# One hybrid trunk on one core: the dt weights' low and high part side by side in one product, and the decay factors of all four chunks by products of 512 columns

## The chip, the cores and the metric

The kernel is one program on one core of a Trainium2 chip. The metric is the device time of one execution in microseconds (us). The core has four engines that compute: TensorE (PE in the rows, with its weight loads shown apart as PEld), VectorE (DVE), ScalarE (ACT) and GpSimd (POOL), and SyncE (SP), which issues the transfers. Each engine works through its own list of instructions in the order in which the scheduler has put them, and waits at an instruction whose operands or whose buffer aren't ready. There are three unprofiled runs and one profiled execution.

## What is computed

The reference is a trunk of two residual layers over 1024 tokens of width 1024. Layer 0 has a state-space mixer (Mamba-2, SSD), layer 1 a causal convolution module, each is followed by a SwiGLU feed-forward part, and a last norm ends the stack. The change is in the mixer:

```python
zxbcdt = u @ w_in
z, xbc, dt = jnp.split(zxbcdt, [D_INNER, D_INNER + CONV_DIM], axis=-1)
...
dt = jax.nn.softplus(dt + dt_bias)            # 32 heads
a = -jnp.exp(a_log)
y = ssd_chunked(xs * dt[..., None], dt * a, bm, cm)
...
# in ssd_chunked, in chunks of 128 tokens
a_cs = jnp.cumsum(a, axis=-1)
lmat = jnp.exp(segsum(a))
y_diag = jnp.einsum("bgrcls,bcsgrp->bclgrp", cb[:, :, None] * lmat, x)
state_decay_out = jnp.exp(a_cs)
y_off = jnp.einsum("bclgn,bcgrpn->bclgrp", cm, states_in) * state_decay_out[..., None]
```

`dt` is one number for each head and token. `state_decay_out`, the decay factors, has to be spread over the 64 channels of a head and multiplied with what the carried state gives.

## The kernel before

All activations lie with channels on the 128 partitions and tokens along the row. The 1024 tokens are two blocks of 512 (`b` = 0, 1), and a block has four chunks of 128 (`z` = 0 to 3). A matrix product is made of rounded parts: `split` (L215) makes a high part (`hi`, by ACT) and the rest (`lo`, by DVE or POOL), and `gemm` (L237) sums `lo*hi`, `hi*lo` and `hi*hi` over slices of 128 input channels, three products of 512 columns for each slice.

The mixer runs in eight steps, one for each block and group of eight heads (`i` = 0 to 7: block `i // 4`, group `i % 4`). `ssd(i)` (L525) gives the list of a step's parts: `prep`, `A(z)` (builds the operands of chunk z and transposes its inputs, `xt`), `B(z)` (two sums of logarithms `sg` on PE, exponentials by ACT, L580, and a mask by DVE, L581, into tiles `EM`), `C(z)` (the chunk's output: state product L601, inner product L609, next state L613, then DVE steps L602 to L629), `t1` and `t2`. `weave` puts the parts of a step between the big products of the next step's input projection and the last step's output projection, so that PE has dense work between them. Out of this the framework's scheduler orders each engine's list by priority and by its own estimate of when an operand is ready.

PSUM has eight banks; in the mixer four (`mm`) hold the big products and four (`ss`) go round for everything small: `sg`, `xt`, the decay factors `eb`, `O`, `Y`, `S`. A bank that comes round again is waited for until its last reader is done.

`dt_path(b)` stands twice, for block 0 at the start and for block 1 in the fill of step 3. It loads the 1024 x 32 weights, splits them in two halves, makes 24 products of 32 output rows (8 slices x 3), multiplies by the norm's factor (block 0 alone, L400), adds the bias (L402), and turns the 32 x 512 result round by four transposes (L405), so that tokens lie on partitions; `dt_post` makes the decay exponents from it. At the start block 0's products take the inputs before the norm (`rhi_b`, `rlo_b`, made by ACT L344 and DVE L345), while the sums of squares (L254, L262) for the norm are still being made.

`decay(z)` (L584) spreads the factors of two chunks: for each of four pairs of heads one product of 256 columns whose weights are 16 rows x 128 (`self.sel`), two to a bank, and a copy by ACT of each bank into `EB` (L593). It is called twice in a step, after `B(0)` for chunks 0 and 1 and after `C(1)` for chunks 2 and 3, and both calls write the same buffer, `c_em[:, 2:4]`; `C(z)` multiplies and adds into it and reads it last at L623. The other half of `c_em` holds two of the three `EM` tiles.

## Time and profile before

| | us |
|---|---|
| three runs: median (lowest, highest) | 2513.57 (2511.85, 2514.39) |
| the profiled execution, its own time | 2513.91 |
| its span, first to last instruction | 2512.2 |
| PE busy in the span | 2488.7 (99%) |
| DVE, ACT, POOL busy | 2038.6, 1281.2, 466.0 |
| mean granted TensorE clock | 0.997 |

The mixer's eight steps take the span from about 80 to 815 us. A row of a timeline gives the start, the time of the row, engine, line, operation, the tiles written and read, rows x columns of the weights and shape, how many instructions stand merged in it, and in brackets how long the engine sat idle before it and what ended that. PE's products overlap: a row of 0.39 us may be followed by the next after 0.23 us, so the cost of a product is read from the difference of two starts. Products in plain fp32 (L601, L609, L613) have two records for each product.

### The profile page before, as it was taken

The numbers are of one execution on the slowest core, as the hardware profiler recorded it, in microseconds if no ns is written. First come the engines' busy times: TensorE is split into PE (matmuls) and PEld (weight loads), VectorE is DVE, ScalarE is ACT, GpSimd is POOL, SyncE is SP. The second block draws the span as 40 slices with busy tenths as digits, with TensorE's granted clock in tenths as the row PEclk, the third lists the DMA queues.
The fourth block names the chain that finished last, engine by engine and source line by source line (L and its number), as shares of the span: only waits on it lengthen the run. The fifth ranks groups of instructions, "written<-read, shape, count | busy, mean of one in ns | idle before, by whom it ended". The sixth has DMA issues, their size and how long they took to land.

```text
span 2512.2 us, 35442 instructions
## 1 busy us (share of the span) xinstructions
PE 2488.7 (99%) x13570; PEld 2108.8 (84%) x13570; DVE 2038.6 (81%) x2998; ACT 1281.2 (51%) x2284; POOL 466.0 (19%) x439
## 2 busy tenths in 40 slices
PE   8999999999999999999999999999999999999998
PEld 5888787887887899998888889988888899899997
DVE  7888989888889886768799578778895787986675
ACT  5665675665666554545332355452323555554443
POOL 3213312112111000000445430004444300000000
PEclk9999999999999999999999999999999999999999
DMA  4222222222223332322223242232232423332322
GB/s 141 84 72 80 76 62 76 76 80 72 76 76 100 92 107 95 109 72 93 98 94 92 95 126 99 68 101 93 98 95 89 129 91 107 130 120 81 120 80 72
DMA packets 71161, 233.50 MB, mean 93 GB/s; under 512 B 7888, under 2 KB 13264, under 8 KB 64080
## 3 DMA queue, kind: packets, MB, share of 16 engines
q1 hardware_dynamic: 70992, 231.25, 28.4%
q8 instruction: 106, 1.74, 0.3%
q14 instruction: 63, 0.52, 0.1%
HBM read 227.02 MB, written 4.19 MB: 92 GB/s over the span
## 4 chain that ended last, share of the span: by engine, by line
PE 96%; DVE 3%; ACT 1%; issue 0%; DMA 0%; POOL 0%; SPq 0%; DVEq 0%; ACTq 0%; POOLq 0%
PE p L241 68%; PE p L773 21%; PE p L609 1%; PE p L613 1%; PE p L601 1%; PE p L576 1%; PE p L564 1%; PE p L577 1%; DVE wlo L217 1%; PE p L592 0%; PE p L288 0%; PE p L544 0%; DVE h L1075 0%; DVE un_s L327 0%; DMA h<-xT 0%
## 5 line engine op out<-in xcount | busy, mean ns | idle before, releaser
L216 ACT ACTIVATE whi<-wst 128x512 fp32r<-128x512 f32 (+3 forms) x676 | 402.6, 597 | 700.4 <-PE p L241 559.5
L241 PE MATMUL p<-uhi_b,wlo 128*128 128x512 f32 x1432 | 571.6, 399 | 1.3 <-ACT uhi_b L216 1.1
L241 PE MATMUL p<-ulo_b,whi 128*128 128x512 f32 x1432 | 564.4, 394 | 1.2 <-POOL ulo_b L217 1.1
L241 PE MATMUL p<-uhi_b,whi 128*128 128x512 f32 x1432 | 562.7, 393 | 0.0
L217 POOL TENSOR_TENSOR wlo<-wst,whi 128x512 fp32r<-128x512 f32 x224 | 286.0, 1277 | 764.9 <-ACT whi L216 764.8
L241 PE MATMUL p<-hid_b,whi 128*128 128x512 f32 x1344 | 418.6, 393 | 0.0
L217 DVE TENSOR_TENSOR wlo<-wst,whi 128x512 fp32r<-128x512 f32 (+2 forms) x452 | 313.1, 695 | 109.3 <-ACT whi L216 105.7
L241 PEld LDWEIGHTS p<-uhi_b,wlo 128*128 128x128 f32 x1432 | 268.7, 188 | 67.9 <-issue 4.0
L241 PEld LDWEIGHTS p<-ulo_b,whi 128*128 128x128 f32 x1432 | 268.8, 188 | 65.4 <-POOL ulo_b L217 2.8
L773 PE MATMUL p<-uhi_b,wh_b 128*128 128x256 f32 x1728 | 323.3, 282 | 0.0
L241 PEld LDWEIGHTS p<-uhi_b,whi 128*128 128x128 f32 x1432 | 269.0, 188 | 61.9 <-issue 0.3
L241 PEld LDWEIGHTS p<-hid_b,whi 128*128 128x128 f32 x1344 | 252.5, 188 | 55.1
L773 PEld LDWEIGHTS p<-uhi_b,wh_b 128*128 128x128 f32 x1728 | 273.1, 190 | 3.2 <-ACT vw_s L800 0.8
L241 PE MATMUL p<-hid_b,wlo 128*128 128x512 f32 x672 | 264.4, 395 | 0.0
L773 PE MATMUL p<-ulo_b,wh_b 128*128 128x256 f32 x864 | 243.4, 282 | 0.0
L773 PE MATMUL p<-tu_b,wh_b 128*128 128x256 f32 x1296 | 171.6, 282 | 0.0
L773 PEld LDWEIGHTS p<-ulo_b,wh_b 128*128 128x128 f32 x864 | 163.7, 189 | 1.9
L773 PEld LDWEIGHTS p<-tu_b,wh_b 128*128 128x128 f32 x1296 | 162.7, 190 | 1.3
L987 DVE SCALAR_TENSOR_TENSOR p<-ci_b,par,p 128x499 f32<-128x499 f32 (+28 forms) x240 | 160.0, 733 | 0.9
L216 ACT ACTIVATE wh_b<-ws_b 128x1024 fp32r<-128x1024 f32 x108 | 114.3, 1060 | 88.9 <-PE p L773 38.0
L989 DVE SCALAR_TENSOR_TENSOR p<-ci_b,par,p 128x512 f32<-128x512 f32 x232 | 158.5, 749 | 0.8
L217 DVE TENSOR_TENSOR wh_b<-ws_b,wh_b 128x1024 fp32r<-128x1024 f32 x108 | 131.3, 1221 | 22.2 <-ACT wh_b L216 21.1
(238 smaller groups left out, 3936.2 us busy)
## 6 DMA issues: line engine op xcount, KB each, us to landing
wq_b<-w_gu SPq DMA_DIRECT2D x54, 1024.0 KB, 4.9
wst<-w_in SPq DMA_DIRECT2D x80, 512.0 KB, 3.5
wst<-w_gu SPq DMA_DIRECT2D x68, 512.0 KB, 3.5
wst<-w_pw SPq DMA_DIRECT2D x48, 512.0 KB, 3.5
wst<-w_dn SPq DMA_DIRECT2D x56, 384.0 KB, 3.2
wst<-w_out SPq DMA_DIRECT2D x64, 256.0 KB, 2.6
wst<-w_dn SPq DMA_DIRECT2D x32, 448.0 KB, 3.4
wst<-w_dn SPq DMA_DIRECT2D x24, 256.0 KB, 2.7
```

The source lines that it names most:

```text
L216: self.nc.scalar.activation(hi, src, AF.Copy)
L217: (eng or self.nc.vector).tensor_tensor(lo, src, hi.bitcast(F32), ALU.subtract)
L241: self.nc.tensor.matmul(acc, a, b, start=n == 0, stop=n == tot - 1)
L564: nc.tensor.transpose(xt[:, zs(j)], self.XS[i][:, j, zs(z)], self.ident)
L576: nc.tensor.matmul(sg, self.gtr, aml, start=True, stop=False)
L577: nc.tensor.matmul(sg, self.gtr, amh, start=False, stop=True)
L601: nc.tensor.matmul(O[:, zs(j)], H[:, zs(j)], CT[:, zs(z)], start=True, stop=True)
L609: nc.tensor.matmul(Y[po:po + 64, zs(hh // 2)], self.XDT[z % 2][:, hh * 64:(hh + 1) * 64], E[:, zs(r)], start=True, stop=True)
L613: nc.tensor.matmul(S, self.BTOK[:, zs(z)], self.XDD[z % 2], start=True, stop=True)
L773: nc.tensor.matmul(to, x, y, start=n == 0 and not more, stop=n == 11, skip_group_check=True)
L987: nc.vector.scalar_tensor_tensor(acc[:, s:], x[:, HALO:TW - s], w(s), acc[:, s:], op0=ALU.mult, op1=ALU.add)
L989: nc.vector.scalar_tensor_tensor(acc if s < 30 else c, x[:, HALO - s:TW - s], w(s), acc, op0=ALU.mult, op1=ALU.add)
```

## The change

For dt, the split weights lie side by side in one tile, 32 columns of low part and 32 of high part, from one ACT and one DVE instruction instead of two and two. Two products for each slice (inputs' low and high part) instead of three give 64 output rows: the upper 32 with the low weights, the lower 32 with the high weights. The factor and the bias are applied to all 64 rows (half the bias to each), and the four transposes become four products with a 64 x 32 matrix of two identities (`id2`), which add both halves. Two DVE instructions at the start make `id2` and the halved bias `hb`.

For the decay factors, `B(0)` is followed by all four pairs: four products of 512 columns, each with a bank and a copy of its own, into the whole of `c_em`. The call after `C(1)` is gone. Two of the `EM` tiles move to a tile of another pool (`em2`), given back after the mixer.

```diff
+        self.hb, self.id2 = ff[:, 1978:1979], ff[:, 1980:2012]
...
+        nc.vector.tensor_tensor(self.id2, self.ident[:, :32], self.ident[:, 32:64], ALU.add)
+        nc.vector.tensor_scalar(self.hb, self.pcol("dt_bias", 0), 0.5, None, op0=ALU.mult)
...
-        self.EM = [self.c_em[:, 0], self.c_em[:, 1], self.c_ms[:, 3]]
-        self.EB = self.c_em[:, 2:4].rearrange("p a (j z l) -> p (a j) z l", z=2, l=P)
+        self.c_e2 = self.half.new("em2")
+        e2 = self.c_e2.rearrange("p (m n) c -> p m (n c)", n=2)
+        self.EM = [e2[:, 0], e2[:, 1], self.c_ms[:, 3]]
+        self.EB = self.c_em.rearrange("p j (z l) -> p j z l", l=P)
...
         def load():
-            st["w"] = self.weight(self.io["w_dt"], 8, 32)
+            w = self.wp.tile([P, 8, P], F32, tag="wst", bufs=2, name=self.nm("wst"))
+            w = w.rearrange("p k c -> p (k c)")[:, :256].rearrange("p (k c) -> p k c", c=32)
+            nc.sync.dma_start(w, self.io["w_dt"])
+            st["w"] = self.wp.tile([P, 4, P], F32R, tag="whi", bufs=4, name=self.nm("whi"))
+            st["w"] = st["w"].rearrange("p k c -> p (k c)").rearrange("p (k c) -> p k c", c=64)
+            self.split(st["w"][:, :, 32:], st["w"][:, :, :32], w)

         def gemm():
             st["acc"] = self.bank("mm")
-            self.gemm(st["acc"][:32], st["w"], self.U[b] if u is None else u)
+            x = [y for hl in (self.U[b] if u is None else u) for y in hl[::-1]]
+            for n, y in enumerate(x):
+                nc.tensor.matmul(st["acc"][:64], st["w"][:, n // 2], y, start=n == 0, stop=n == 15)
...
-            nc.vector.tensor_tensor(raw[:32], acc[:32], fac[:32], ALU.mult)
+            nc.vector.tensor_tensor(raw[:64], acc[:64], fac[:64], ALU.mult)
...
-        nc.vector.tensor_scalar(raw[:32], acc[:32], self.par[:32, o:o + 1], None, op0=ALU.add)
+        nc.vector.tensor_scalar(raw[:64], acc[:64], self.hb[:64], None, op0=ALU.add)
...
-            nc.tensor.transpose(tp[:, z * 32:(z + 1) * 32], raw[:32, z * P:(z + 1) * P], self.ident[:32, :32])
+            nc.tensor.matmul(tp[:, z * 32:(z + 1) * 32], raw[:64, z * P:(z + 1) * P], self.id2[:64],
+                             start=True, stop=True)
...
-        def decay(z):
-
-            w = slice(z * P, (z + 2) * P)
-            for a in range(2):
+        def decay(a):
+
+            gp = slice(32 * g, 32 * g + 16)
+            for j in (2 * a, 2 * a + 1):
                 eb = self.bank("ss")
-                for j in range(2):
-                    gp = slice(32 * g, 32 * g + 16)
-                    lt = self.sel.rearrange("p q c -> p (q c)")[gp, zs(2 * a + j)]
-                    nc.tensor.matmul(eb[:, 2 * P * j:2 * P * (j + 1)], lt, self.er[gp, w], start=True, stop=True)
-                nc.scalar.activation(self.c_em[:, 2 + a], eb, AF.Copy)
+                nc.tensor.matmul(eb, self.sel.rearrange("p q c -> p (q c)")[gp, zs(j)], self.er[gp], start=True, stop=True)
+                nc.scalar.activation(self.c_em[:, j], eb, AF.Copy)
...
-            EB = self.EB[:, :, z % 2]
+            EB = self.EB[:, :, z]
...
-        steps = [prep, lambda: A(0), lambda: (B(0), decay(0)), lambda: A(1)]
+        steps = [prep, lambda: A(0), lambda: (B(0), decay(0), decay(1)), lambda: A(1)]
         for z in range(NZ):
-            steps.append(lambda z=z: (C(z), decay(2)) if z == 1 else C(z))
+            steps.append(lambda z=z: C(z))
```

On PE, at `B(0)` of step 0, the list of before has the two `sg` sums (`am_b,sr_b`), the four decay products of chunks 0 and 1 (`sr_b` alone) and then the big products of the next projection (`uhi_b`, `ulo_b`):

```order
L577 MATMUL p_92_837<-am_b_91,sr_b_65 128x512
L592 MATMUL p_93_842<-sr_b_65 128x256 x2
L592 MATMUL p_94_846<-sr_b_65 128x256 x2
L241 MATMUL p_95_850<-uhi_b_245,wlo_737 128x512
L241 MATMUL p_95_850<-ulo_b_246,whi_736 128x512
```

The list of the changed kernel at the same place, where L592 and L593 are now the sums, L605 the decay products and L244 the big products:

```order
L593 MATMUL p_89_827<-am_b_91,sr_b_65 128x512
L605 MATMUL p_90_832<-sr_b_65 128x512
L605 MATMUL p_91_835<-sr_b_65 128x512
L244 MATMUL p_94_844<-uhi_b_235,wlo_727 128x512
L244 MATMUL p_94_844<-ulo_b_236,whi_726 128x512
L605 MATMUL p_92_838<-sr_b_65 128x512
L244 MATMUL p_94_844<-uhi_b_235,whi_726 128x512
L244 MATMUL p_94_844<-uhi_b_235,wlo_727 128x512
L244 MATMUL p_94_844<-ulo_b_236,whi_726 128x512
L244 MATMUL p_94_844<-uhi_b_235,whi_726 128x512
L605 MATMUL p_93_841<-sr_b_65 128x512
L244 MATMUL p_94_844<-uhi_b_235,wlo_727 128x512
```

The four products now stand in three places between dense products: two together, one, one. So it is in six of the eight steps; in steps 3 and 7 three stand together and one apart. In the whole program the decay products stand in 22 places, in the list of before in 19.

On ACT, at the same place of step 0, before has the two exponentials (L580) with a convolution step (L483) between them, the two copies of decay factors (L593), and operands of `A(1)` and weights (`whi`) after them:

```order
L580 ACTIVATE em_b_92<-p_91_832 128x512
L483 ACTIVATE v_s_815<-sf_b_64 128x512
L580 ACTIVATE em_b_92<-p_92_837 128x512
L593 ACTIVATE em_b_92<-p_93_842 128x512
L593 ACTIVATE em_b_92<-p_94_846 128x512
L560 ACTIVATE am_b_91<-sf_b_64,sr_b_65 128x128 x2
L216 ACTIVATE whi_887<-wst_885 128x512
```

In the changed kernel the exponentials are L596 and the copies L606:

```order
L596 ACTIVATE em_x_97<-p_88_822 128x512
L499 ACTIVATE v_s_805<-sf_b_64 128x512
L596 ACTIVATE em_x_97<-p_89_827 128x512
L606 ACTIVATE em_b_92<-p_90_832 128x512
L606 ACTIVATE em_b_92<-p_91_835 128x512
L606 ACTIVATE em_b_92<-p_92_838 128x512
L606 ACTIVATE em_b_92<-p_93_841 128x512
L219 ACTIVATE whi_881<-wst_879 128x512
```

Two copies more stand ahead of the weights; the two that stood behind `C(1)` are gone.

On PE, in step 3, where block 1's dt product is, the list of before has products of 32 output rows, a pair of decay products among them, and the inner products of `C(1)` (L609):

```order
L577 MATMUL p_439_3375<-am_b_91,sr_b_65 128x512
L241 MATMUL p_469_3556<-ulo_b_3278,whi_3514 32x512
L592 MATMUL p_454_3494<-sr_b_65 128x256 x2
L241 MATMUL p_469_3556<-uhi_b_3277,whi_3514 32x512
L241 MATMUL p_469_3556<-uhi_b_3277,wlo_3515 32x512
L241 MATMUL p_469_3556<-ulo_b_3278,whi_3514 32x512
L241 MATMUL p_469_3556<-uhi_b_3277,whi_3514 32x512
L241 MATMUL p_469_3556<-uhi_b_3277,wlo_3515 32x512
L241 MATMUL p_469_3556<-ulo_b_3278,whi_3514 32x512
L241 MATMUL p_469_3556<-uhi_b_3277,whi_3514 32x512
L609 MATMUL p_451_3470<-ms_b_96,xd_b_93 64x128 x4
L609 MATMUL p_451_3470<-em_b_92,xd_b_93 64x128 x4
```

In the changed kernel (L406 the dt products, L622 the inner products) they are of 64 rows, with no decay product among them:

```order
L593 MATMUL p_438_3357<-am_b_91,sr_b_65 128x512
L406 MATMUL p_463_3525<-uhi_b_3259,whi_3488 64x512
L406 MATMUL p_463_3525<-ulo_b_3260,whi_3488 64x512
L406 MATMUL p_463_3525<-uhi_b_3259,whi_3488 64x512
L406 MATMUL p_463_3525<-ulo_b_3368,whi_3488 64x512
L406 MATMUL p_463_3525<-uhi_b_3367,whi_3488 64x512
L406 MATMUL p_463_3525<-ulo_b_3368,whi_3488 64x512
L406 MATMUL p_463_3525<-uhi_b_3367,whi_3488 64x512
L406 MATMUL p_463_3525<-ulo_b_3368,whi_3488 64x512
L592 MATMUL p_455_3491<-am_b_91,sr_b_65 128x512
L622 MATMUL p_450_3452<-ms_b_96,xd_b_93 64x128 x4
L622 MATMUL p_450_3452<-em_x_97,xd_b_93 64x128 x4
```

The inner products stand behind 13 of the 16 dt products and three of the sums, before behind 12 of the 24, two sums and a pair of decay products.

## Rows read from the trace of the kernel before

**Rows 1.** The page: busy time, share of the span and instructions of each engine; and the chain of work that ended last, its shares by engine.
```profile
PE 2488.7 (99%) x13570; PEld 2108.8 (84%) x13570; DVE 2038.6 (81%) x2998; ACT 1281.2 (51%) x2284; POOL 466.0 (19%) x439
...
PE 96%; DVE 3%; ACT 1%; issue 0%; DMA 0%; POOL 0%; SPq 0%; DVEq 0%; ACTq 0%; POOLq 0%
```

**Rows 2.** Waits of PE over the whole span: the instruction that waited, what it waited for, us in total, times, longest.
```profile
PE p L241 <- DVE rlo_b L345: 3.0, 5, 1.0
...
PE p L241 <- ACT uhi_b L216: 1.1, 1, 1.1
...
PE p L564 <- ACT em_b L593: 1.0, 1, 1.0
PE p L576 <- DVE ms_b L545: 0.9, 1, 0.9
...
PE p L592 <- DVE xd_b L570: 0.3, 1, 0.3
PE p L609 <- DVE ms_b L581: 0.3, 1, 0.3
```

**Rows 3.** Busy time by stretch of the span, all engines: the stretch and its length, PE, PEld, DVE, ACT and POOL busy (instructions), PE's granted clock (1.00 is 2.4 GHz, 0.50 is 1.2 GHz), DMA share, GB/s.
```profile
9.70:13.00 3.30, 2.84 (x6) 0.71 (x6) 3.30 (x8) 2.78 (x6) 1.54 (x1) 0.50 1.04 416
...
40.40:43.70 3.30, 3.30 (x11) 2.27 (x10) 3.08 (x6) 0.00 (x0) 2.15 (x2) 0.50 0.12 50
...
82.00:820.00 738.00, 734.91 (x3720) 587.27 (x3719) 643.16 (x958) 467.77 (x978) 154.19 (x162) 1.00 0.24 77
```

**Rows 4.** Timeline at the start: PE at three of its waits (block 0's dt product twice, the first normalized inputs once), and DVE at one step of the sum of squares.
```profile
15.59 0.42 PE L241 MATMUL p<-rlo_b,whi 128*32 128x512 f32 x1 [0.96 <-DVE rlo_b L345]
...
20.68 0.43 PE L241 MATMUL p<-rlo_b,whi 128*32 128x512 f32 x1 [0.92 <-DVE rlo_b L345]
...
39.41 0.49 PE L241 MATMUL p<-uhi_b,wlo 128*128 128x512 f32 x1 [1.14 <-ACT uhi_b L216]
...
19.27 0.69 DVE L262 TENSOR_TENSOR ssum_s<-ssum_s,sq_s 128x512 f32<-128x512 f32 x1 [1.19 <-POOL ssum_s L262]
```

**Rows 5.** Timeline of step 3: PE in block 1's dt product and at the inner products behind it, and DVE at what these waited for.
```profile
388.82 0.39 PE L241 MATMUL p<-uhi_b,wlo 128*32 128x512 f32 x1
389.05 0.40 PE L241 MATMUL p<-ulo_b,whi 128*32 128x512 f32 x1
389.28 0.39 PE L241 MATMUL p<-uhi_b,whi 128*32 128x512 f32 x1
...
390.69 0.66 PE L609 MATMUL p<-ms_b,xd_b 128*64 128x128 f32 x8 [0.32 <-DVE ms_b L581]
...
389.96 0.68 DVE L581 TENSOR_TENSOR ms_b<-ms_b 128x512 f32<-128x512 f32 x1
```

**Rows 6.** Timeline of step 3 a little later: PE at the transposes of `A(3)`, ACT at the square that stands ahead of the decay copies and at these copies, DVE at two steps of `C(1)` (L620 reads `Y`, L623 reads `EB` last).
```profile
398.20 0.66 PE L564 MATMUL p<-ident,xs_b 128*128 128x128 f32 x4 [0.97 <-ACT em_b L593]
...
397.04 0.63 ACT L627 ACTIVATE gsq_s<-sz_b 128x512 f32<-128x512 f32 x1 [1.12 <-DVE sz_b L623]
397.57 1.06 ACT L593 ACTIVATE em_b<-p 128x512 f32<-128x512 f32 x2
...
392.36 0.67 DVE L620 TENSOR_TENSOR em_b<-em_b,p 128x512 f32<-128x512 f32 x1
...
396.08 0.93 DVE L623 TENSOR_TENSOR sz_b<-sz_b,em_b 128x512 f32<-128x512 f32 x1
```

**Rows 7.** Timeline of PE around decay products: four of them in step 0, and two of them in step 7.
```profile
91.48 0.40 PE L577 MATMUL p<-am_b,sr_b 128*128 128x512 f32 x1
91.80 0.73 PE L592 MATMUL p<-sr_b 16*128 16x256 f32 x4
92.47 0.50 PE L241 MATMUL p<-uhi_b,wlo 128*128 128x512 f32 x1
92.80 0.39 PE L241 MATMUL p<-ulo_b,whi 128*128 128x512 f32 x1
93.03 0.40 PE L241 MATMUL p<-uhi_b,whi 128*128 128x512 f32 x1
...
786.01 0.40 PE L241 MATMUL p<-yl_b,whi 128*128 128x512 f32 x1
786.33 0.50 PE L592 MATMUL p<-sr_b 16*128 16x256 f32 x2
786.76 0.51 PE L241 MATMUL p<-yh_b,whi 128*128 128x512 f32 x1
787.10 0.39 PE L241 MATMUL p<-yh_b,wlo 128*128 128x512 f32 x1
```

**Rows 8.** Timeline of PE: the four transposes of dt in block 1, and the four fp32 state products of a chunk (two records each, 128 columns).
```profile
402.69 0.44 PE L405 MATMUL p<-ident,dtraw_s 32*128 32x32 f32 x4
...
112.92 1.06 PE L601 MATMUL p<-bct_b,H_b 128*128 128x128 f32 x8
```

**Rows 9.** Timeline of ACT behind the two sums of step 0: exponentials, a convolution step, copies of decay factors.
```profile
91.99 0.59 ACT L580 ACTIVATE em_b<-p 128x512 f32<-128x512 f32 x1
92.47 0.81 ACT L483 ACTIVATE v_s<-sf_b 128x512 f32<-128x512 f32 x1
93.17 0.60 ACT L580 ACTIVATE em_b<-p 128x512 f32<-128x512 f32 x1
93.65 1.09 ACT L593 ACTIVATE em_b<-p 128x512 f32<-128x512 f32 x2
```

More of the change, by code (lines that the diff above doesn't have):

```diff
@@ L384, in dt_path @@
     def dt_path(self, b, u=None, fac=None):
+        nc = self.nc
         st = {}
         def load():
-            st["w"] = self.weight(self.io["w_dt"], 8, 32)
+            w = self.wp.tile([P, 8, P], F32, tag="wst", bufs=2, name=self.nm("wst"))
[4 more added lines that the diff above has]
+            self.split(st["w"][:, :, 32:], st["w"][:, :, :32], w)
         def gemm():
             st["acc"] = self.bank("mm")
-            self.gemm(st["acc"][:32], st["w"], self.U[b] if u is None else u)
+            x = [y for hl in (self.U[b] if u is None else u) for y in hl[::-1]]
+            for n, y in enumerate(x):
+                nc.tensor.matmul(st["acc"][:64], st["w"][:, n // 2], y, start=n == 0, stop=n == 15)
         return [Unit(gemm, load), Unit(lambda: self.dt_pre(b, st["acc"], fac)), Unit(lambda: self.dt_post(b))]
@@ L1121, in run @@
             q += weave(self.ssd(i), fill) + post
-        q += [Unit(lambda: self.big.drop(*self.mix_bigs)), call(self.phase, 8)]
+        q += [Unit(lambda: (self.big.drop(*self.mix_bigs), self.half.drop(self.c_e2))), call(self.phase, 8)]
         fast = lambda *a, **k: self.ffn(*a, fast=True, **k)
```

## The prediction

> **What bounds the kernel now.** I read the page's busy times and chain first, then PE's waits, then the stretches, then the timeline at each place that the diff touches. PE is busy for 99% of the span and carries 96% of the chain that ended last [rows 1]. Between 82 and 820 us, which holds the mixer, it is busy 734.91 of 738.00 us, while DVE has 643 and ACT 468 [rows 3]. So in the mixer a product that goes away is time gained, and a change on DVE or ACT counts only where PE comes to wait for it. The list of PE's waits is short: about 3 us for `rlo_b` and 1.1 us for `uhi_b`, both at the start, and in the mixer single waits of 0.3 to 1.0 us [rows 2]. Two of these, at L564 and L592, are at the change. The exception is the start: there PE stands at 15.59 and 20.68 for DVE's `rlo_b`, and at 39.41 for ACT's `uhi_b` [rows 4].
>
> **Part 1, block 1's dt product (step 3).** Sixteen products take the place of 24. One costs 0.23 us, the difference of the starts 388.82, 389.05 and 389.28 [rows 5] with 32 columns of weights, and 0.23 with 128 (92.80 to 93.03 [rows 7]), so I take 0.23 for 64 too. Eight fewer: -1.84 us, on a path where PE has no cover to lose.
>
> **Part 2, block 0's dt product (start).** Eight fewer there as well, but PE is waiting between them: each pair of products needs one `rlo_b` from DVE, and at 15.59 and 20.68 it sat idle 0.96 and 0.92 us for it [rows 4]. DVE itself waits in the sum of squares (1.19 us at 19.27, for POOL), and that chain, not PE, leads to the norm and to the `uhi_b` for which PE waits 1.14 us at 39.41. The dropped products only lengthen idle time: 0. The two added DVE instructions (two small tiles) end before that 1.19 us of DVE idle time, which covers them; uncovered they would cost a few tenths. Bounds for the part: -1.84 (all gained) and +1.7 (the clock, rival C).
>
> **Part 3, four transposes become four fp32 products of 64 rows, twice.** The four transposes take 0.44 us as a row [rows 8]. No row has an fp32 product of 32 columns. From below: no more than now, 0. From above: as long as the four fp32 products of 128 columns, 1.06 us, so +0.62 each time. Those have two records for each product where a transpose has one. I take two passes of what is one now, about 0.06 us more for each of four, +0.25 us; twice, +0.5 us. Both stand where PE is dense afterwards.
>
> **Part 4, the decay products on PE.** A place with four products of 256 columns takes PE from 91.48 to 92.80, that is 1.32 us, of which two ordinary products are 0.46: 0.86 us. A place with two takes from 786.01 to 787.10, 1.09 less 0.46: 0.63 us [rows 7]. So two products cost 0.23 us, 0.115 each, and going into the 16-row shape and out again costs 0.40 us a place, however many stand in it (the product before is followed after 0.32 to 0.33 instead of 0.23, the first dense one after 0.34). A product of 512 columns in this shape isn't in the trace; at the least it is what dense ones take, 0.23, at the most two of 256, 0.23 also, so there is little to choose. Before: 64 x 0.115 + 19 x 0.40 = 14.96 us. After, with the 22 places that the order has: 32 x 0.23 + 22 x 0.40 = 16.16 us. That is +1.2 us. Against it goes the wait at L592 for `xd_b`, 0.35 us at most by [rows 2], which I tie to the call after `C(1)` in step 7 (its bank came round late): -0.3. Sum +0.9 us. So joining two products into one gains nothing, and scattering them loses.
>
> A rule of the Trainium skill would say otherwise of the joining: TensorEngine Tiling (Array Packing), in Performance Considerations, gives each product an overhead of some 60 cycles. As an estimate from that page, at 2.4 GHz, 32 fewer products would save 0.8 us more, and the time forecast below would be 2511.8. The rows speak against it here: two of 256 cost no more than one of 512.
>
> **Part 5, the call after `C(1)` disappears.** Its copies wrote a buffer which DVE was still reading. In step 3 they stood on ACT behind a square that waited 1.12 us for L623 (396.08 to 397.0), ran at 397.57, and PE stood at the transposes of `A(3)` 0.97 us for the bank that they emptied [rows 6]. In the new order of banks these transposes take the bank of `Y`, free after L620 at 393.0. The wait goes: -0.97 us; a further wait in its place would be for L620, and by 393.0 that is early enough. The other 0.9 us wait, at L576 for L545, is ahead of the change and stays.
>
> **Part 6, a wait that grows.** In step 3 the inner products waited 0.32 us for L581, which DVE began at 389.96, held by other work [rows 5]. With 13 instead of 12 dt products, one sum more and two pairs of decay products fewer ahead of them, PE is there some 0.8 us earlier. If L581 comes no earlier, all of that is waited: +0.8; if ACT's new order brings it forward by as much, 0. I take the middle, +0.4 us.
>
> **Part 7, ACT.** As many copies as before, but all four behind the exponentials. Two new copies of about 0.5 us (two took 1.09) stand ahead of the next weights' split, 1.1 us later at worst. The weights have two sets of buffers, and in the whole list from which [rows 2] are taken PE never waits for `whi` or `wlo`, so nothing. The third decay product needs the bank of the first sum, empty when its exponential ends at 92.58; the fourth that of the second, 93.77 [rows 9]. By the order the third comes at about 93.1 and the fourth at about 94.55, so each has 0.5 to 0.8 us to spare. Cost 0; what it takes without that cover is rival B.
>
> **Sum.** -1.84 + 0 + 0.5 + 0.9 - 0.97 + 0.4 = -1.0 us. Against the profiled execution's own 2513.91 that is 2512.9; it lies 0.34 above the median of the runs, so against 2513.57 I forecast 2512.6, 0.04% less. In step 7's end the scheduler has also cut some small groups apart and put others together; with the sizes above that is 0.8 us either way, and I leave it in the range.
>
> **Rivals.**
>
> A, the first product counts as well. For it: it is eight products, and the low clock from 40.40 to 43.70 [rows 3] comes after a stretch of waits that an earlier PE could shorten. Against: the waits there are for DVE, ACT and POOL [rows 4]. It would give -1.84 more, and half of 3.3 us, 1.65, if that low stretch goes: 2509.1, and 2508.2 with parts 3 and 6 at their lower ends. Chance 0.13.
>
> B, slower: the four banks. All four are taken by two sums and two decay products when the third and fourth come, and PE's list can't pass them; everything dense behind waits for ACT. It decides from the point where an exponential ends more than 0.5 to 0.8 us later than in [rows 9], in all steps. To end 0.2% above before it must cost 6 us, 0.75 us a step; the time would be 2519. Against it: ACT is half idle, and steps 3 and 7 have no convolution step between the exponentials. Chance 0.06.
>
> C, the clock at the start. From 9.70 to 13.00 it was granted at 0.50, with PE busy 2.84 of 3.30 us on six products before it rose [rows 3]; after the change two thirds of these remain in the same time. If it then stays at 1.2 GHz for another such stretch, 1.65 us of PE's pace are lost, of which the idle 0.96 and 0.92 us [rows 4] cover most; uncovered it is 2514.2. Chance of the uncovered price 0.13. The Trainium skill's TensorE: Matmul & The Clock Gate, Part 1, says that the low clock is the default and that activity releases it; by that rule the rise would come later after this change, and the trace agrees so far as its rise follows a busy stretch.
>
> D, the gain of step 3 doesn't last. DVE and ACT set the pace there: part 6 costs its 0.8 and another wait takes the place of part 5's 0.97: 2512.6 + 0.4 + 0.97 = 2514.0. Chance 0.15.
>
> **How the numbers follow.** My forecast has 0.53. A run of this kernel can be told from no change beyond about 0.2%, 5 us: faster is under 2508.5, slower over 2518.6. The forecast, C and D lie within. Of A, whose two times lie on both sides of the border, I count 0.08 as faster and 0.05 as within. Faster 0.12, within 0.2% 0.80, slower 0.08; 0.04 of the first and 0.02 of the last are for what I haven't thought of. The range goes down to 2508.5 (A without the lower ends) and up to 2515.5 (D with step 7's 0.8 and part 3's upper end), which leaves out some 2 in 10.
>
> **What would show it.** The dt products' rows: 16 at 0.23 us in step 3. Decay products: 32 of 512 columns with 22 places at 0.4 us over the dense pace; a place with one product at 0.63 us proves part 4, at 0.25 refutes it. L564's wait for L593 gone; L609's wait for L581 in step 3 at 0.3 to 1.1 us. At the start PE still idle at `rlo_b` and at `uhi_b` near 39.4. A wait of the decay products for the exponentials, step after step, would prove B and the forecast wrong; a granted clock of 0.50 after 13.1 us would prove C.

## The result: 0.22% slower, and runs that scatter

The changed kernel takes 2517.55 us in the median of 22 runs, the kernel before 2512.9 in 22, that is 4.65 us less. One run of the changed kernel, at 13854.28 us, is a slow one and stands outside the ratio and all that follows. The ratio of the means is 1.0022, interval 1.0016 to 1.0028. The forecast was 2512.6 with a range up to 2515.5, so the time lies outside. The runs of before lie between 2511.39 and 2514.39; those of the changed kernel begin at 2513.32 and reach 2524.7. Its nine runs above 2519 us have mean granted clocks of 0.992 to 0.994, the twelve others 0.995 to 0.998. The profiled execution took 2515.16 us, span 2513.3; it is one of the shorter ones.

The page after: busy times, and the chain by engine. PE's share of the chain falls from 96% to 94% and DVE's rises from 3% to 4% [rows 1].

```profile
PE 2490.1 (99%) x13530; PEld 2106.9 (84%) x13530; DVE 2038.8 (81%) x2998; ACT 1282.0 (51%) x2282; POOL 465.8 (19%) x439
...
PE 94%; DVE 4%; ACT 1%; issue 0%; POOL 0%; DMA 0%; SPq 0%; DVEq 0%; ACTq 0%; POOLq 0%
```

Waits of PE in the mixer after (us in total, times, longest). The waits at the transposes for the decay copies and at the decay products for `xd_b` [rows 2] are gone; 1.2 us at the next-state product (L626, which was L613 in before) and 0.6 us in step 7 have come.

```profile
PE p L626 <- DVE xd_b L586: 1.2, 1, 1.2
PE p L592 <- DVE ms_b L561: 0.9, 1, 0.9
PE p L592 <- ACT uhi_b L219: 0.6, 1, 0.6
PE p L622 <- DVE em_x L597: 0.4, 1, 0.4
```

Stretches after, columns as in [rows 3]. The clock column is what matters: in the mixer, where the trace of before has no stretch below 1.00, there is now one at 0.50, that is at 1.2 GHz. The row of the whole mixer doesn't show it: a mean over 738 us, it reads 1.00 as it did in before.

```profile
8.40:18.60 10.20, 7.94 (x17) 3.86 (x18) 9.03 (x22) 8.71 (x16) 4.40 (x2) 0.50 0.82 298
40.40:43.70 3.30, 3.30 (x19) 2.69 (x18) 3.30 (x6) 0.63 (x1) 1.77 (x4) 1.00 0.00 0
82.00:820.00 738.00, 734.47 (x3671) 582.72 (x3670) 640.78 (x953) 467.71 (x976) 152.52 (x162) 1.00 0.24 76
400.90:404.30 3.40, 2.20 (x12) 1.38 (x12) 2.42 (x5) 0.00 (x0) 0.00 (x0) 1.00 0.46 153
404.30:407.70 3.40, 3.40 (x9) 2.63 (x10) 3.28 (x8) 0.83 (x2) 0.19 (x1) 0.50 0.00 1
407.80:411.20 3.40, 3.40 (x17) 2.78 (x16) 1.95 (x3) 0.63 (x1) 0.00 (x0) 1.00 0.00 0
```

PE's timeline in step 3 around it: the second half of the inner products, one dense product, the wait, the fp32 next-state product, the turn of dt (L420), and then dense products that follow one another after 0.43 us instead of 0.23. In before, the turn of dt and this step's wait, which was then at the transposes, lay 4.5 us apart with dense products between them [rows 6, 8].

```profile
399.92 0.61 PE L622 MATMUL p<-ms_b,xd_b 128*64 128x128 f32 x8
400.46 0.49 PE L244 MATMUL p<-uhi_b,wlo 128*128 128x512 f32 x1
402.15 1.10 PE L626 MATMUL p<-xd_b,ms_b 128*128 128x512 f32 x2 [1.20 <-DVE xd_b L586]
403.18 1.08 PE L420 MATMUL p<-sf_b,dtraw_s 64*128 64x32 f32 x8
404.18 0.70 PE L244 MATMUL p<-ulo_b,whi 128*128 128x512 f32 x1
404.68 0.63 PE L244 MATMUL p<-uhi_b,whi 128*128 128x512 f32 x1
405.11 0.63 PE L244 MATMUL p<-uhi_b,wlo 128*128 128x512 f32 x1
```

The timeline of PE at the parts that were priced: two dt products of step 3, 0.23 us apart; and a decay product by itself in step 0 (compare [rows 5, 7]). From 90.92 to 92.01 are 1.09 us, less two ordinary products (0.46) 0.63 for this place.

```profile
386.12 0.39 PE L406 MATMUL p<-ulo_b,whi 128*64 128x512 f32 x1
386.35 0.40 PE L406 MATMUL p<-uhi_b,whi 128*64 128x512 f32 x1
...
90.92 0.40 PE L244 MATMUL p<-ulo_b,whi 128*128 128x512 f32 x1
91.25 0.50 PE L605 MATMUL p<-sr_b 16*128 16x512 f32 x1
91.67 0.50 PE L244 MATMUL p<-uhi_b,whi 128*128 128x512 f32 x1
92.01 0.40 PE L244 MATMUL p<-uhi_b,wlo 128*128 128x512 f32 x1
```

To see where time comes and goes I take the starts of the same dense product of projections and feed-forward in two traces (both have 12216) and subtract that of before. Numbers are us; a column is the product that starts at that time in before.

| kernel | 82 | 200 | 296 | 383 | 480 | 830 | 2499 |
|---|---|---|---|---|---|---|---|
| after | -1.87 | -1.32 | -0.91 | +0.28 | +0.74 | +0.92 | +0.93 |
| after_again | -1.37 | -0.81 | -0.25 | +0.99 | +3.14 | +3.36 | +3.47 |
| dt_both | -1.38 | -1.38 | -1.25 | -1.21 | -2.58 | -2.31 | -2.29 |
| decay_only | -1.11 | -0.58 | -0.01 | +1.20 | +0.93 | +1.14 | +1.22 |
| after_fill | -1.49 | -0.90 | +2.64 | +3.88 | +2.86 | +3.05 | +3.09 |
| plug23 | -2.55 | -1.99 | +1.69 | +2.92 | +2.48 | +2.70 | +2.75 |
| before_long | -2.25 | -2.19 | +2.09 | +2.13 | +2.15 | +2.14 | +2.28 |
| full_before | +1.09 | +0.26 | -0.24 | -0.69 | -0.61 | -3.00 | -2.60 |
| full_after | +2.76 | +3.85 | +3.38 | +3.94 | +1.80 | -0.70 | -0.60 |

Behind 830 us no row changes by more than 0.4. The columns 200 and 296 stand beside decay products that the lists place differently, so there a difference can shift by about 1.2 us from one product to the next. In after the start gains 1.9, then each stretch loses. The gain at the start is an execution's, not the change's: before_long, whose start is that of before, gains 2.25 there (by [rows 3] the low stretch at 40 us alone, missing in both, is worth up to 1.65).

### The profile page after: what moved, and what is told of

Same layout as the page of the kernel before. It is cut to its first block, busy times and chain, and to the rows that moved or that the text cites. A ratio compares the mean times of both kernels' runs of the same rounds, so it can differ in the third digit from the quotient of the medians.

```text
span 2513.3 us, 35345 instructions
## 1 busy us (share of the span) xinstructions
PE 2490.1 (99%) x13530; PEld 2106.9 (84%) x13530; DVE 2038.8 (81%) x2998; ACT 1282.0 (51%) x2282; POOL 465.8 (19%) x439
## 4 chain that ended last, share of the span: by engine, by line
PE 94%; DVE 4%; ACT 1%; issue 0%; POOL 0%; DMA 0%; SPq 0%; DVEq 0%; ACTq 0%; POOLq 0%
PE p L244 66%; PE p L786 21%; PE p L622 1%; PE p L626 1%; PE p L614 1%; DVE wlo L220 1%; PE p L592 0%; PE p L605 0%; PE p L593 0%; PE p L580 0%; PE p L291 0%; DVE v_s L501 0%; DVE un_s L330 0%; PE p L560 0%; DVE h L1088 0%
## 5 line engine op out<-in xcount | busy, mean ns | idle before, releaser
L219 ACT ACTIVATE whi<-wst 128x512 fp32r<-128x512 f32 (+2 forms) x674 | 402.4, 598 | 703.1 <-PE p L244 555.1
L244 PE MATMUL p<-uhi_b,wlo 128*128 128x512 f32 x1424 | 569.3, 400 | 1.6 <-ACT uhi_b L219 1.5
L244 PE MATMUL p<-ulo_b,whi 128*128 128x512 f32 x1424 | 561.7, 395 | 1.2 <-POOL ulo_b L220 1.1
L244 PE MATMUL p<-uhi_b,whi 128*128 128x512 f32 x1424 | 559.8, 393 | 0.0
L244 PE MATMUL p<-hid_b,whi 128*128 128x512 f32 x1344 | 418.7, 393 | 0.0
L220 DVE TENSOR_TENSOR wlo<-wst,whi 128x512 fp32r<-128x512 f32 (+1 forms) x448 | 315.6, 706 | 108.8 <-ACT whi L219 105.4
L244 PEld LDWEIGHTS p<-uhi_b,wlo 128*128 128x128 f32 x1424 | 268.1, 188 | 69.7 <-issue 7.6
L244 PEld LDWEIGHTS p<-ulo_b,whi 128*128 128x128 f32 x1424 | 267.9, 188 | 64.8 <-issue 3.3
L244 PEld LDWEIGHTS p<-uhi_b,whi 128*128 128x128 f32 x1424 | 268.0, 188 | 62.0 <-issue 1.6
L244 PEld LDWEIGHTS p<-hid_b,whi 128*128 128x128 f32 x1344 | 252.4, 188 | 55.2
L244 PE MATMUL p<-hid_b,wlo 128*128 128x512 f32 x672 | 264.4, 395 | 0.0
```

What stands on the lines that cost most here:

```text
L219: self.nc.scalar.activation(hi, src, AF.Copy)
L220: (eng or self.nc.vector).tensor_tensor(lo, src, hi.bitcast(F32), ALU.subtract)
L244: self.nc.tensor.matmul(acc, a, b, start=n == 0, stop=n == tot - 1)
```

## The experiments

"Before" is always the median of the runs of before that stood beside a kernel on its chip. The 95% interval of a ratio reaches some 0.09% to either side, 2.2 us, so a difference below that is not clear of none.

**The two parts alone, and the two dt products alone.** Edits: the lines of the change for dt without those for the decay factors (dt_both), the other way round (decay_only), and dt_both for one block:

```diff
-            w = self.wp.tile([P, 8, P], F32, tag="wst", bufs=2, name=self.nm("wst"))
+            if b != 0:    # dt_first; dt_second has 1
+                st["w"] = self.weight(self.io["w_dt"], 8, 32)
+                return
```

> The kernel before with the dt products of both blocks changed and the decay products as they were. The changed kernel's runs go from 2513.3 to 2524.7 us where those of before go from 2511.4 to 2514.4, and long runs show a lower mean granted clock. Theory S (stretches of low clock that come in some runs only, caused by the first dt product at the start) and theory U (the same, caused by the second dt product and the fp32 turn in step 3): median 2515 to 2518, runs spread over 6 us or more. Theory E (the decay products, scattered over more places, cause them): 2511.5 to 2513, spread 3 us, since eight products fewer in step 3 save 1.84 and two turns by fp32 products cost 1.3.

> The kernel before with the decay products changed and the dt products as they were. Theory E: median 2515 to 2519, runs spread over 6 us or more, mean clock down to 0.993 in the long ones. Theories S and U: 2513 to 2515 (scattering the products costs 1 to 2 us on PE), spread 3 us like before.

> The kernel before with block 0's dt product alone changed, at the start. Theory S: median 2515 to 2517, spread 6 us or more, low clock after 13 us or after 43 us in the profile. Theories U and E: 2512 to 2514, spread 3 us.

> The kernel before with block 1's dt product alone changed, in step 3. Theory U: median 2514 to 2517, spread 6 us or more, low clock between 390 and 420 us in the profile, as in the changed kernel's profile at 404.31 to 407.72. Theories S and E: 2511 to 2513 (sixteen products instead of 24 save 1.84, the fp32 turn costs 0.64), spread 3 us.

Measured, before 2513.39: dt_both 2511.99 (-1.40), decay_only 2515.39 (+2.00), dt_first 2514.12 (+0.73), dt_second 2512.32 (-1.07). No profile of the four has a low clock between 45 and 2500 us. The parts add up to +0.6, near the changed kernel's shortest runs (+0.4), and 4 us short of its median. Three of eleven runs of dt_first (2517.4 to 2517.7) and one of dt_both (2516.35) stand 2.9 and 2.2 us above the next one; the longest of decay_only (2517.6) is 2.2 above its median, as the longest run of before there is above its own. So no theory of the three has it alone: neither part has the changed kernel's scatter of 11 us, the two together have it. The same holds for the 1.2 us wait at the next-state product of step 3: it is in the profile of neither dt_both nor decay_only.

**The same kernel again; more work at the start; the turn by transposes.** after_again has no edit. after_fill:

```diff
             for n, y in enumerate(x):
+                if b == 0 and n % 2 == 0:
+                    nc.tensor.matmul(d[:64], st["w"][:, n // 2], x[n + 1], start=True, stop=True)
                 nc.tensor.matmul(st["acc"][:64], st["w"][:, n // 2], y, start=n == 0, stop=n == 15)
```

after_turn:

```diff
-            nc.tensor.matmul(tp[:, z * 32:(z + 1) * 32], raw[:64, z * P:(z + 1) * P], self.id2[:64],
-                             start=True, stop=True)
+            nc.tensor.transpose(tp[:, z * 64:(z + 1) * 64], raw[:64, z * P:(z + 1) * P], self.ident[:64, :64])
...
-        nc.vector.tensor_copy(v, tp[:, :128])
+        nc.vector.tensor_copy(v3, t4[:, :, 0])
+        nc.vector.tensor_tensor(v3, v3, t4[:, :, 1], ALU.add)
```

> The changed kernel once more, beside the others on one chip. If its scatter belongs to the kernel: median 2516 to 2519, highest above 2520, mean clock in the long runs 0.992 to 0.994. If it belonged to the executions of that other time: median 2513 to 2515 (the two parts alone sum to +0.6 us over before), highest under 2518.

> The changed kernel with eight products put back into block 0's dt product, whose result nobody reads (high weights by high inputs, into a bank of its own, ahead of each pair), so that PE is as busy at the start as before. Theory S (PE too idle at the start, low clock lasting longer there in some runs): median 2513 to 2515, spread 3 to 4 us, mean clock not under 0.996. Theory U (low clock from the fp32 turn and the wait in step 3): as the changed kernel, 2516 to 2519 with runs above 2520.

> The changed kernel with the two turns of dt by transposes of 64 rows (tokens by 64 columns) and DVE adding the halves, in place of fp32 products. By the measured 1.00 us for four fp32 products against 0.36 for four transposes it saves 1.0 to 1.3 us at the medians. Theory U: the low clock at 404 goes and the scatter with it, median 2512 to 2514. Theory S: scatter as in the changed kernel, median 2515 to 2517.

Measured, before 2513.15: 2517.20 (2515.0 to 2523.2), 2517.16 (2516.6 to 2524.1, in seven runs) and 2517.92 (2514.0 to 2520.6). The scatter belongs to the kernel. Theory S falls: with as much work at the start as before it stays. Theory U falls in its first form: without the fp32 turn it stays. The turn itself is shorter, 0.39 us from 406.93 to 407.32 against 1.00, yet the median isn't. What the three profiles give is the place: after_again has its low clock from 404.6 to 411.4, as after in step 3; the other two have it from 266.3 and 267.0 on, in step 2, for 6.8 us. The table shows the price: after_fill loses 3.5 us between 200 and 296 where after loses 0.4. Two executions of one kernel show it too: between 383 and 480, where after_again is at 1.2 GHz for 6.8 us and after for 3.4, the one loses 2.15 us and the other 0.46. The row of after_again:

```profile
404.60:411.40 6.80, 6.80 (x19) 5.47 (x19) 3.58 (x9) 1.46 (x3) 0.19 (x1) 0.50 0.06 25
```

**Filling PE's waits.** plug3 puts three dense products ahead of the waiting next-state product of step 3; plug23 also makes the first sum of `B(0)` in step 2 three times over, where PE waits 1.0 us.

```diff
                 S = self.bank("ss")
+                if i == 3 and z == 2:
+                    for _ in range(3):
+                        nc.tensor.matmul(S, self.gtr, self.U[1][0][0], start=True, stop=True)
...
-                nc.tensor.matmul(sg, self.gtr, aml, start=True, stop=False)
-                nc.tensor.matmul(sg, self.gtr, amh, start=False, stop=True)
+                for _ in range(1 + 2 * (i == 2 and z == 0 and q == 0)):
+                    nc.tensor.matmul(sg, self.gtr, aml, start=True, stop=False)
+                    nc.tensor.matmul(sg, self.gtr, amh, start=False, stop=True)
```

> The changed kernel with three dense products of 512 columns put ahead of the state product of C(2) in step 3, where PE waits 1.2 us for DVE; they write its bank, which the state product then overwrites. Theory M (a low clock follows where a PE wait stands among decay, fp32 and transposing products with hardly a dense one between; in step 3 at 400 to 404, in step 2 at 263 to 267; each takes 1.7 or 3.4 us, in runs of its own): no low clock at 404 to 412, median 2514.5 to 2516, some runs still above 2517 for step 2. Rival N (the low clock is not tied to these places): as the changed kernel, 2517 and scatter to 2523.

> The same, and the first sum of B(0) in step 2 made three times over (four more dense products where PE waits 1.0 us for DVE). Theory M: no low clock between 45 and 2500 us, median 2513 to 2515, highest under 2517. Rival N: 2517 and scatter.

Measured, before 2512.88: plug3 2518.25 (2514.5 to 2522.3), plug23 2516.23 (2513.8 to 2517.8). The first filling missed its aim: the timeline of plug3 shows that the added products themselves wait for the bank, whose last reader is DVE's L586, so the idle time stands where it stood. And yet this profile has no low clock there; it has it in step 2.

```profile
406.44 0.93 PE L628 MATMUL p<-uhi_b,sr_b 128*128 128x512 f32 x3 [1.22 <-DVE xd_b L586]
407.21 1.02 PE L629 MATMUL p<-xd_b,ms_b 128*128 128x512 f32 x2
...
267.00:273.80 6.80, 6.80 (x15) 4.36 (x15) 3.99 (x7) 1.63 (x4) 0.26 (x2) 0.50 0.14 41
404.00:411.00 7.00, 5.78 (x38) 4.10 (x35) 6.59 (x13) 1.49 (x3) 0.19 (x1) 1.00 0.23 75
```

The second filling worked, and refuted theory M. In plug23 PE has no wait in step 2 (stretches, then its timeline), and yet the clock falls, behind the decay products of 16 rows. Its scatter is half of plug3's, so the wait may still have a share.

```profile
262.90:266.30 3.40, 3.13 (x9) 1.32 (x9) 3.40 (x6) 3.07 (x6) 2.19 (x3) 1.00 0.17 60
266.40:273.10 6.70, 6.70 (x15) 4.97 (x16) 4.43 (x7) 3.83 (x11) 0.10 (x1) 0.50 0.15 39
```

```profile
263.11 0.50 PE L593 MATMUL p<-am_b,sr_b 128*128 128x512 f32 x1
263.45 0.39 PE L594 MATMUL p<-am_b,sr_b 128*128 128x512 f32 x1
263.77 1.09 PE L606 MATMUL p<-sr_b 16*128 16x512 f32 x2
264.79 0.50 PE L244 MATMUL p<-uhi_b,wlo 128*128 128x512 f32 x1
265.13 0.39 PE L244 MATMUL p<-ulo_b,whi 128*128 128x512 f32 x1
265.46 0.49 PE L606 MATMUL p<-sr_b 16*128 16x512 f32 x1
265.88 0.49 PE L244 MATMUL p<-uhi_b,whi 128*128 128x512 f32 x1
266.30 0.78 PE L606 MATMUL p<-sr_b 16*128 16x512 f32 x1
...
267.61 0.63 PE L244 MATMUL p<-ulo_b,whi 128*128 128x512 f32 x1
```

**More 16-row products in before.** In the kernel before, the four decay products of step 2's first call are made four times each.

```diff
+                    for _ in range(4 if i == 2 and z == 0 else 1):
                         nc.tensor.matmul(eb[:, 2 * P * j:2 * P * (j + 1)], lt, self.er[gp, w], start=True, stop=True)
```

> The kernel before with the four decay products of chunks 0 and 1 in step 2, behind the 0.93 us wait, made four times over each (12 more products of 256 columns and 16 rows, 1.4 us at 0.115). Theory M with 16-row products counting little for the clock: low clock behind 266 us in most runs, median 2516 to 2518, spread 4 us or more. Rival N, or 16-row products counting like dense ones: 2514 to 2515, spread 3 us.

Measured: 2514.74 (+1.86; 2512.9 to 2516.9). The median lies where rival N had it (2514 to 2515): the twelve added products alone are worth 1.4 us at 0.115, so the low clock can't have cost the median run much. The profile is of one of the two longest runs (2516.20 us). It has the low clock, in a place where no profile with before's decay products had it, and the table shows its 4.3 us between 200 and 296. It begins while the sixteen products run, which take 3.04 us, 0.19 each:

```profile
263.27 3.11 PE L593 MATMUL p<-sr_b 16*128 16x256 f32 x16
266.31 0.80 PE L241 MATMUL p<-uhi_b,wlo 128*128 128x512 f32 x1
...
260.80:264.10 3.30, 2.23 (x13) 1.39 (x12) 3.30 (x6) 2.80 (x5) 1.72 (x2) 1.00 0.28 79
264.20:270.90 6.70, 6.70 (x22) 5.51 (x21) 5.38 (x8) 3.29 (x8) 0.96 (x3) 0.50 0.12 42
```

**All four decay products in one place.** after_ahead puts them ahead of the sums; ahead_apart does so in all steps but step 2, with both fillings, the turn by transposes, and block 1's turn two projections later.

```diff
-        steps = [prep, lambda: A(0), lambda: (B(0), decay(0), decay(1)), lambda: A(1)]
+        steps = [prep, lambda: A(0), lambda: (decay(0), decay(1), B(0)), lambda: A(1)]
...
-dtp[:1] + ip[:1] + dtp[1:2] + ip[1:]
+dtp[:1] + ip[:3] + dtp[1:2] + ip[3:]
```

> The changed kernel with the four decay products ahead of the two sums of B(0) instead of behind them, so that all four of a step stand in one place: 8 places with 4 products of 512 columns instead of 22. By part 4's price (0.40 us a place, 0.23 a product) their cost falls from 17.0 to 8 x 1.32 = 10.6 us: 6.4 us less than the changed kernel on the same chip, 2509 to 2512 with its scatter. Rival: the four copies by ACT keep the banks that the sums need next, PE waits up to 0.8 us in each step, and all of it is given back: 2515 to 2518.

> The changed kernel with the decay products ahead of the sums in all steps but step 2 (10 places instead of 22), the turn by transposes, the turn of block 1 two projections later, away from C(2), and both fillings of plug23. Theory M and part 4's price: 5.8 us less for the places, 0.6 to 1.3 for the turn, no low clock in the mixer: 2506.5 to 2509, highest under 2512, so under the kernel before by 0.2% or more. Rival N: 2509 to 2513 with scatter. Against it: waits that the new places bring, as the 1.1 and 0.6 us in step 2 of the run with all steps ahead.

Measured: after_ahead 2512.99 (-0.16), that is 4.2 less than after_again beside it; ahead_apart 2511.25 (-1.63). Part 4's price holds: a place of four takes from 90.04 to 91.81, 1.77, less 0.46: 1.31 us, and 0.40 + 4 x 0.23 is 1.32. Of the 6.4 us two thirds arrive; in its profile some go into new waits, 1.3 us at L291 ahead of step 1 (0.3 in after) and 0.6 more in step 2. ahead_apart misses theory M's 2506.5 to 2509 and lies where rival N had it, and both kernels' profiles still have the low clock in step 2 (from 267.4 and 268.4).

```profile
90.04 0.39 PE L244 MATMUL p<-uhi_b,whi 128*128 128x512 f32 x1
90.36 1.19 PE L605 MATMUL p<-sr_b 16*128 16x512 f32 x4
91.48 0.50 PE L244 MATMUL p<-uhi_b,wlo 128*128 128x512 f32 x1
91.81 0.40 PE L244 MATMUL p<-ulo_b,whi 128*128 128x512 f32 x1
```

**128 rows instead of 16.** The decay products take all rows; a POOL instruction in each step sets the selection of the other groups to zero. PE's order is the same, instruction by instruction.

```diff
+            nc.gpsimd.tensor_tensor(self.selm, self.sel.rearrange("p q c -> p (q c)").bitcast(F32),
+                                    self.mask[:, g:g + 1].to_broadcast([P, 512]), ALU.mult)
...
-                nc.tensor.matmul(eb, self.sel.rearrange("p q c -> p (q c)")[gp, zs(j)], self.er[gp], start=True, stop=True)
+                nc.tensor.matmul(eb, self.selm[:, zs(j)], self.er, start=True, stop=True)
```

> The changed kernel with all decay products on 128 rows instead of 16: their weights are the same selection with zeros in the rows of the other groups (made by one POOL instruction in each step's first part), the moving operand is the whole tile. PE's order and columns are the same. Theory R (16 rows, not idle time alone, bring the low clock, and the 0.40 us of a place come from going into the 16-row shape and out): the places fall from 17.0 to 32 x 0.23 = 7.4 us, no low clock at 263 to 273, at most the one at 404 is left; median 2504 to 2507 against 2517. Theory M (the idle time alone brings the low clock, and a change of operands alone costs the 0.40): 2516 to 2518 with scatter.

> The kernel before with the decay products on 128 rows, PE's order the same. Theory R: 15.9 us for the places fall to 64 x 0.115 = 7.4, median 2504 to 2506. Theory M: 2512 to 2514.

> full_after with the turns by transposes and block 1's turn two projections later, away from C(2). Theory R and the low clock in step 3 from the gathering of fp32 products, turn and wait: 2502 to 2505, spread 4 us or less, no low clock between 45 and 2500 us. Theory M: 2513 to 2516.

> The kernel before with the dt products changed (as in dt_both, 2511.99) and the decay products on 128 rows, 256 columns, in the two calls of before. Theory R: 8.5 us less than dt_both, 2502 to 2505. Theory M: 2511 to 2513.

Measured, before 2512.73: full_after 2513.42 (+0.69, where the changed kernel has +4.0 to +4.7), full_before 2510.07 (-2.66), full_apart 2510.74 (-1.99), full_dt 2508.39 (-4.34). In the rows theory R holds: most of the places' price is gone, and the clock stays up in step 2. In the times it doesn't: all four lie below theory M's ranges, but 3.4 to 6.4 us above those of theory R. Timeline of full_after in step 2: the 1.00 us wait is still there, with all four decay products behind it, and the clock stays at 1.00; a single place in step 0 takes from 95.16 to 95.96, 0.80, less 0.46: 0.34 with a product that is itself 0.23.

```profile
268.91 0.50 PE L603 MATMUL p<-am_b,sr_b 128*128 128x512 f32 x1 [1.00 <-DVE ms_b L572]
...
269.49 0.39 PE L616 MATMUL p<-sr_b 128*128 128x512 f32 x1
270.20 0.47 PE L616 MATMUL p<-sr_b 128*128 128x512 f32 x1 [0.32 <-DVE xd_b L597]
...
95.16 0.40 PE L253 MATMUL p<-ulo_b,whi 128*128 128x512 f32 x1
95.39 0.49 PE L616 MATMUL p<-sr_b 128*128 128x512 f32 x1
95.73 0.39 PE L253 MATMUL p<-uhi_b,whi 128*128 128x512 f32 x1
95.96 0.40 PE L253 MATMUL p<-uhi_b,wlo 128*128 128x512 f32 x1
...
266.40:273.10 6.70, 5.38 (x23) 3.80 (x22) 6.70 (x11) 4.92 (x9) 3.17 (x4) 1.00 0.17 46
```

The median single place is 0.26 against 0.63 in after. In neither of the two profiles with 128 rows and the changed order (full_after, full_apart) does the clock fall in step 2; with 512-column products of 16 rows it fell there in six of nine. The other profiles with 128 rows (full_before, full_dt and two below) have the order of before, in which it stayed up with 16 rows as well. So this supports theory R and doesn't prove it. Where the rest of the expected gain went the table says in part: full_before is 1.1 us late at 82 us, where the instructions that make the mask have taken DVE 0.7 us between 22 and 23 us and the low clock lasted 6.9 us from 10.7 on (3.4 in before), and full_after 2.8, with a low clock from 41.1 to 47.9 in its profile. Then both gain, but PE comes to wait for DVE: in full_before 1.5 us once at the inner products and 1.1 in three waits for `xd_b`, where there were 0.3 and 0.3. full_after still scatters over 5 us (2510.0 to 2515.3); what remains of its scatter isn't settled. It has a new wait of 2.4 us at L300 ahead of step 1, and in full_apart, which has it too, a low clock follows it (157.7 to 161.1).

**The best of it.** full_dt with the turn by transposes, and then with block 1's turn two projections later.

> full_dt (2508.39) with the two turns of dt by transposes of 64 rows and a DVE addition in place of fp32 products. The turn's rows fall from 1.00 to about 0.4 us each. If they lie on PE's path: 2507.2 to 2507.8; if waits for DVE beside them take the place: 2508.4.

> full_dt_turn with block 1's turn two projections later, away from C(2) of step 3. If the gathering there still costs (low clock or waits in some runs): median down by up to 1 us and the highest under 2510; if not, as full_dt_turn within 0.5 us.

Measured, before 2512.97: 2508.63 (-4.34) and 2507.89 (-5.08; ratio 0.9981, interval 0.9972 to 0.9990). The shorter turn gains nothing in the median beside full_dt's -4.34. In the profiles the stretch from 82 to 830 us is 0.7 us shorter, and the start 0.8 us longer: full_dt's execution has no low clock there, that of full_dt_turn 13.6 us of it. Moving the turn gives 0.7 in the median, which is within the scatter; in the profiles that stretch differs by less than 0.1 us, so the gain of the move is not shown. Neither profile has a low clock in the mixer. This last kernel beats both, by 5 us and by 10.

## Why the prediction was wrong, point by point

- **Part 1** was right: sixteen products 0.23 us apart, and dt_second gives -1.07, near -1.84 and a turn 0.64 longer, though not clear of no change.
- **Part 2** fits with 0: dt_first has +0.73, near its turn's 0.64, with an interval that includes no change. The low clock at the start did last longer in the profile, up to 18.6 instead of 13.0 us as rival C said, but under PE's waits for `rlo_b`, and the first norm was not late. Its length is an execution's as well: decay_only, with the old dt product, has 6.8 us of it, full_dt, with the new one, none.
- **Part 3** was mis-sized: 1.00 us instead of 0.36 for the four, +0.64 each time, the upper bound that I had and didn't take. That is 0.8 us of the miss.
- **Part 4** was right in its price: 0.63 us for a place with one product. The 22 places take 17.0 us, the 19 of before 15.85, of which 0.35 are the wait in step 7 that went. So it is +1.5 for a predicted +1.2, and +1.16 with the wait for +0.9. The Trainium skill's TensorEngine Tiling (Array Packing) says under Key Properties that changing the tiling mode drains the engine; full_after agrees so far as with all rows the extra 0.40 us falls to 0.03 in the median single place. The 60 cycles for each product that the same page of the Trainium skill has under Performance Considerations don't show: a place with two products of 512 columns takes 0.86 us in after, one with four of 256 took 0.86 in before.
- **Part 5** named the right wait and it went; but what came next was not early enough. The next-state product of `C(2)`, pulled forward, waits 1.20 us for L586. That is rival D's second half, with 1.20 in place of its 0.97.
- **Part 6**: no wait at the inner products of step 3. The 0.4 us for `em_x`, in step 7, is the only one like it. **Part 7** was right, and rival B didn't happen: PE waits nowhere for exponentials.
- **What failed** is the mixer's clock, a term that the sum put at nothing on a row that can't show it. I read [rows 3] as saying that the mixer runs at 2.4 GHz, carried that over to the changed kernel, and asked for the clock only at the start. But the row is a mean over 738 us, and it reads 1.00 after the change too. All eight profiles of kernels with both parts of the change and 16 rows have a stretch at 1.2 GHz in the mixer, six in step 2 and two in step 3; those of before, dt_both, dt_first, dt_second and decay_only have none. It costs 1.6 us (404.3 to 407.7, eight products at 0.43 instead of 0.23) or 3.1 (after_fill). Without it the kernel would, as an estimate from the parts and from its shortest runs, be at +0.4 to +0.6: still not the forecast -1.0, mostly because of parts 3 and 5.

In the profiled execution the mixer from 82 to 830 us loses 2.8: -1.84 for the dt products, +0.64 for the turn, +1.5 for the places, +0.5 for the waits (3.4 instead of 2.9), +1.6 for the low clock make 2.4, and 0.4 is not assigned, within the 0.8 that I had left for groups cut apart.

Why the clock falls is not settled. For step 2 the 16 rows are the best supported cause: plug23 has the fall without the wait, before_long has it with twelve more such products, full_after and full_apart keep 1.00 with the wait. But each of these is one execution, and three of nine profiles with 16 rows and 512 columns kept the clock there as well. For step 3 the cause is only read off the timeline: the filling missed, and full_apart and full_dt_apart changed the rows as well. The same wait and turn stand in after_fill, after_ahead, plug3 and full_after, whose clock stays up in step 3. Why some executions of the changed kernel exceed 2520 us was not seen in a profile; two falls in one execution would give it, and their mean clocks of 0.992 to 0.994 fit more time at 1.2 GHz.

## What to carry to other kernels

A small product that uses few rows cost more than its columns here: 0.40 us for going into its shape and out of it. Zeros in the unused rows took nearly all of that away, at the price of one POOL instruction in each step and four small DVE instructions at the start; and no profile with them has a low clock in step 2. And a single profile can miss a loss that depends on the execution: run it several times, compare the spread as well as the median, and look at the clock of each short stretch, since a mean over a long one hides it.

## What was not expected of the hardware

In plug23 PE was busy 3.13 of 3.40 us, partly with products of 16 rows, and the granted clock fell behind it; in before it was busy 2.25 of 3.30 us at the same place, with products of 16 rows too, and the clock stayed at 1.00:

```profile
263.10:266.40 3.30, 2.25 (x10) 1.13 (x8) 3.30 (x6) 3.03 (x6) 1.96 (x2) 1.00 0.27 79
266.40:273.20 6.80, 6.80 (x33) 5.66 (x33) 6.48 (x11) 4.71 (x13) 0.82 (x3) 1.00 0.18 50
```

The Trainium skill's TensorE: Matmul & The Clock Gate, Part 1, lets the clock follow how busy the engine is; the busy share that these rows show doesn't tell which of the two falls. Four fp32 products of 64 rows and 32 columns take 1.00 us, as much as four of 128 rows and 128 columns [rows 8], while four transposes of 64 rows take 0.39.
